# Five buffered weight pieces before each norm, the inversion's matrix in another pool, and later sums behind the mixer

## The chip, the cores and the metric

The kernel runs on one core of a Trainium2 chip. The metric is the device time of one execution in microseconds (us), taken as the median over runs; lower is better.

## What is computed

A decoder trunk of two layers works on 264 tokens: one prompt of 256 and eight samples of one token each, in float32, 1024 channels wide. Each layer is

```python
h = LN1(alpha*x + 0.5*SwiGLU_1(x))
h = LN2(alpha*h + W_out [DeltaNet(h) | Pool(h)])
x = LN3(alpha*h + 0.5*SwiGLU_2(h))
```

A SwiGLU has gate and up matrices of 1024 x 2816 and a down matrix of 2816 x 1024. The mixer projects `h` with one matrix (q, k, v, z, pooling input and two small gates), runs a gated delta rule in exact chunked form (which needs the inverse of a triangular matrix per head and chunk) beside a causal pooling, and projects both with `W_out`. States of the samples are read and written.

## The kernel before, in words

**Products.** Channels lie on the partitions and the 264 tokens along the free dimension. A float32 product is made of three matmuls per block of 128 channels (`mm3`, lines 218 to 222): each weight piece of 128 output channels is split into a rounded high part and a low remainder, each activation likewise, and high x high, high x low and low x high are summed. A piece has 8 blocks, so 24 matmuls.

**Weights.** `Weights` (line 139) holds an ordered list of units. A unit is one load of 1 MB on SP's queue into a buffer `wraw` (three of them) and holds two pieces. ScalarE writes a piece's high part (`whi`, L179) and VectorE the low part (`wlo`, L184). Three pieces have buffers in the pool `wpool` (`WB = 3`). Four more (`XB = 4`) have buffers `xhi0`, `xlo0` and so on in the pool `xp` at the right end of the memory, which is open only from the end of one stage to the start of the next. The list of units (lines 206 to 215) says which units ahead of a norm use them: the first two gate/up units (not in the very first SwiGLU) and the first two units of `w_in`. `W.ahead(n)` loads until n pieces are ready or on their way; `W.after` and `W.after_hi` name an instruction behind which the planner has to put the next low and high parts.

**Norms.** Ahead of a norm's result the next stage already works: `RH` and `RL` are high and low parts of the unnormalised rows times the gain, and `raw_products` (line 399) multiplies them with the first pieces. `Norm.stats` (line 335) sums over channels on TensorE from two accumulators `acc1`, `acc2`; `normalise` (line 355) then subtracts the mean (L360), multiplies by the reciprocal deviation (L363), scales (L365) and makes `HH` (L367) and `HL` (L375), which all later products read. `settle` (line 416) corrects the early products with mean and deviation. In the first SwiGLU of the second layer and in both SwiGLUs behind a mixer there are six early products; in these last two the order on TensorE is: three products up to block 5, the sums of `stats`, the fourth product up to block 5, then blocks 6 and 7 of all four, then the fifth and sixth products, and then a pair of products on `HH` and `HL`. In a mixer the four k pieces are early, and the pair (first q, last pooling group) with the small gates follows on `HH` and `HL`.

**Behind the mixer.** The loop at line 1244 makes the eight tiles of `W_out` and calls `norm.add`, which at high priority adds the tile to `X` (L332), makes squares (L267), `RH` (L269), `RL` (L270) and the running sums on VectorE (L277, L278, L280, L282).

**Order of the work.** TensorE runs in program order. On the other engines a planner orders the instructions by a simulation: of those that are ready, the one with the higher priority, and then the one that comes first in the program, goes first. The order is fixed when the kernel is built, and each engine then waits at its next instruction. SP's loads are one such queue.

**Pools.** `ffn` opens a pool `fp` with `gh` and `gl`, 22 rows each, whose widths and offsets come from `ROWS`. The mixer has a pool `mp`, and, once `xp` is closed, a pool `mp2` at the right end, in the place of `xp`. `MT`, the matrix to be inverted (6 KB per partition), is in `mp`; its place serves `uw` later. Buffers of one pool that reuse memory of another wait for its last user, tile by tile.

Of the kernel before, what the change touches and what calls it, by code (L numbers as in the profile page):

```python
# [9 lines left out]
F32 = mybir.dt.float32  # L10
F32R = mybir.dt.float32r
AF = mybir.ActivationFunctionType
ALU = mybir.AluOpType
# [3 lines left out]
P = 128  # L17
# [8 lines left out]
H = 4  # L26
# [6 lines left out]
WB = 3  # L33
XB = 4
SB = 3
ROWS = ((320, 0), (288, 0), (320, 16), (272, 0))
IDLE = 18
# [53 lines left out]
def trunk(ctx: ExitStack, tc: tile.TileContext, a: dict):  # L91
# [30 lines left out]
    def tables(name):  # L122
        tc.keep_in_program_order(nc.scalar.preload_act_table_set(name))
# [84 lines left out]
    for l in range(DEPTH):  # L208
        for n in ("f1", "f2"):
            for m in range(KF):  # L210
                units.append((a[n + "_gu"][l, m], 2 * m if m < 2 and (l, n) != (0, "f1") else None))
            units += [(a[n + "_d"][l, i], None) for i in range(KF // 2)]
            if n == "f1":
                units += [(a["w_in"][l, i], 2 * i if i < 2 else None) for i in range(10)]
                units += [(a["w_out"][l, i], None) for i in range(4)]
# [24 lines left out]
    class Norm:  # L240
# [4 lines left out]
        def __init__(self, l, which, eps, fold=True):  # L245
            self.l, self.eps, self.fold = l, eps, fold
            c = S_LN + 16 * which
            self.c = c
            self.g = lambda m: sm[:, l, c + m:c + m + 1]
            self.b = lambda m: sm[:, l, c + 8 + m:c + 9 + m]  # L250
            self.acc1 = lpool.tile([P, T], F32, name="acc1", tag="acc1")
            self.acc2 = lpool.tile([P, T], F32, name="acc2", tag="acc2")
            self.shift = None

        def columns(self):
# [6 lines left out]
        def shifted(self, m, eng1, eng2):  # L262
            y = X[:, m, :]
            sq = lpool.tile([P, T], F32, name="sq", tag="sq", bufs=4)
            late = self.fold and m > 5
            if not late:
                nc.scalar.activation(sq, y, AF.Square)  # L267
            if self.fold:
                self.rh_op = nc.scalar.activation(RH[:, m, 0:T], y, AF.Copy, scale=self.g(m))  # L269
                self.rl_op = nc.vector.scalar_tensor_tensor(RL[:, m, 0:T], y, self.g(m), RH[:, m, 0:T].bitcast(F32),  # L270
                                                            ALU.mult, ALU.subtract)
            if late:
                nc.scalar.activation(sq, y, AF.Square)
# [54 lines left out]
        def add(self, m, ps):  # L328
            if m == 0:
                self.columns()  # L330
            with tc.high_priority():
                nc.vector.tensor_add(X[:, m, :], ps, X[:, m, :])  # L332
                self.shifted(m, nc.vector, nc.vector)

# [20 lines left out]
        def normalise(self):  # L355
# [6 lines left out]
            for n, y in enumerate(pairs):  # L362
                nc.vector.tensor_mul(y, y, by2(self.rstd))  # L363
                for m in (2 * n, 2 * n + 1):
# [60 lines left out]

    def ffn(src, norm, xnext, rows, late=False):
        with tc.tile_pool(name="fp", bufs=1, reuse_waits="tile") as fp:
            rs, room = rows
            if room:
                fp.tile([P, room], F32, name="room")  # L430
            gh, gl = ([fp.tile([P, rs], F32R, name=f"{n}{m}")[:, 0:T] for m in range(KF)] for n in ("gh", "gl"))

# [13 lines left out]
            if src is not None:  # L446
# [3 lines left out]
                                                 [((0, 1), 0, 4), None, ((0, 1), 4, KD), ((2, 3), 0, KD), ((4, 5), 0, KD)])  # L450
                W.after, W.after_hi = src.rstd_op, src.exp_op
                src.normalise()
                tables("silu_and_others")
                W.ahead(2)
# [40 lines left out]
    def mixer(l, src, norm, xstack):  # L495
        with tc.tile_pool(name="mp", bufs=1, reuse_waits="tile") as mp:
# [51 lines left out]
            src.normalise()  # L548
            kr = [k_raw(p) for p in pk_]
            xstack.close()  # L550
            W.xp = None
# [69 lines left out]


            W.ahead(2)
            wq, wp = W.get(), W.get()
            pq, pp, pba = (psa.tile([P, T], F32, name=n, tag="ax") for n in ("pq", "pp", "pba"))
            for k in range(KD):
                nc.tensor.matmul(pba, wb[:, k, :], HH[:, k, :], start=k == 0, stop=False)
                nc.tensor.matmul(pba, wb[:, k, :], HL[:, k, :], start=False, stop=k == KD - 1)
                mm3(pq, wq, k, HH[:, k, :], HL[:, k, :], k == 0, k == KD - 1)
                mm3(pp, wp, k, HH[:, k, :], HL[:, k, :], k == 0, k == KD - 1)  # L630
            bar = mp.tile([8, 3 * P], F32, name="bar")
# [124 lines left out]

            MT = mp.tile([P, H, 3 * P], F32, name="MT")

# [443 lines left out]
            sf = mp.tile([P, NB, P], F32, name="sf", tag="S", bufs=SB)[:, 0:H]  # L1202
            uw = mp.tile([P, 2, H, P], F32, name="uw", tag="MT")
            for b in range(2):
# [84 lines left out]
    for l in range(DEPTH):  # L1289
        n1 = Norm(l, 0, 4.0 * LN_EPS)  # L1290
        ffn(src, n1, True, ROWS[2 * l])
        n2 = Norm(l, 1, LN_EPS)
        mixer(l, n1, n2, xstack)
        src = Norm(l, 2, 4.0 * LN_EPS, l < DEPTH - 1)
        ffn(n2, src, l < DEPTH - 1, ROWS[2 * l + 1], True)
    src.stats()
# [93 lines left out]
```

## Time and profile before

| | us |
|---|---|
| median of 3 runs | 1102.72 |
| lowest, highest | 1101.37, 1105.08 |
| the profiled execution, its own time | 1104.32 |
| its span, first to last instruction | 1102.2 |
| TensorE busy in it | 1049.1 |
| VectorE busy | 766.0 |
| ScalarE busy | 581.8 |

TensorE is busy for 95% of the span. It stands for some 14 us at the end, behind the last matmul, and for the rest in short gaps around the norms and within the mixers. A busy share is an average over stages: the SwiGLUs keep TensorE busy without a gap, while near the norms VectorE is full for stretches of 15 to 20 us.

### The profile page before, as it was taken

Reading aid. Unit: us, or ns where it says so; the run is one execution under the profiler, and the core shown is the slowest. Engines: PE = TensorE matmul, PEld = TensorE weight load, DVE = VectorE, ACT = ScalarE, POOL = GpSimd, SP = SyncE. Lnnn points to the kernel's source line nnn. Section 1 sums busy time; section 2 is a strip of 40 time slices with the busy share of each in tenths; the row PEclk is TensorE's granted clock in tenths of the full one; section 3 lists DMA queues with packets and bytes.
Section 4 is the critical chain, followed back from the end, with each engine's and each line's share of the span. In section 5 each row is a group of like instructions: output and inputs, shape, how many; then the busy total and the mean of one; then the engine's idle time right before and its main releaser. Section 6 shows DMA issues by size and latency. Waiting matters only on the chain.

```text
span 1102.2 us, 20763 instructions
## 1 busy us (share of the span) xinstructions
PE 1049.1 (95%) x8410; PEld 1034.9 (94%) x8410; DVE 766.0 (70%) x1226; ACT 581.8 (53%) x1017; POOL 208.0 (19%) x248
## 2 busy tenths in 40 slices
PE   8999999989898999999999999999799989999995
PEld 8999999988898999999999999998789989999994
DVE  5555567899789855557775555778997897555554
ACT  5444445657546644445564444456564466444432
POOL 0000022244940000004100000322567200000132
PEclk9999999999999999999999999999899999999998
DMA  8455445642224354554615455565331344554441
GB/s 305 181 190 188 171 178 199 228 147 98 100 115 181 117 186 179 189 190 165 257 63 205 169 178 190 191 241 170 128 118 47 146 163 158 187 192 176 169 154 40
DMA packets 35872, 183.24 MB, mean 166 GB/s; under 512 B 6848, under 2 KB 12608, under 8 KB 15552
## 3 DMA queue, kind: packets, MB, share of 16 engines
q1 hardware_dynamic: 28704, 175.19, 43.7%
q10 hardware_dynamic: 7072, 6.72, 1.8%
q8 instruction: 66, 1.08, 0.4%
q14 instruction: 30, 0.25, 0.1%
HBM read 175.18 MB, written 6.72 MB: 165 GB/s over the span
## 4 chain that ended last, share of the span: by engine, by line
PE 79%; DVE 11%; ACT 5%; POOL 3%; issue 1%; DMA 1%; ACTq 0%; DVEq 0%
PE pd L221 8%; PE pd L220 8%; PE pd L222 8%; PE pu L222 7%; PE pg L221 7%; PE pg L222 7%; PE pu L220 7%; PE pu L221 7%; PE pg L220 7%; DVE wlo L184 2%; ACT X L365 2%; POOL X L326 1%; DVE c L525 1%; ACT whi L179 1%; ACT HH L367 1%
## 5 line engine op out<-in xcount | busy, mean ns | idle before, releaser
L184 DVE TENSOR_TENSOR wlo<-wraw,whi 128x1024 fp32r<-128x1024 f32 (+1 forms) x306 | 374.1, 1226 | 214.7 <-ACT whi L179 214.0
L179 ACT ACTIVATE whi<-wraw 128x1024 fp32r<-128x1024 f32 (+1 forms) x306 | 317.6, 1041 | 337.6 <-issue 115.0
L221 PE MATMUL pd<-gl,whi 128*128 128x264 f32 x704 | 199.5, 283 | 0.0
L220 PE MATMUL pd<-gh,whi 128*128 128x264 f32 x704 | 199.2, 283 | 0.0
L222 PE MATMUL pd<-gh,wlo 128*128 128x264 f32 x704 | 199.2, 283 | 0.0
L220 PE MATMUL pu<-HH,whi 128*128 128x264 f32 x632 | 180.5, 286 | 3.1 <-ACT whi L179 3.1
L222 PE MATMUL pu<-HH,wlo 128*128 128x264 f32 x632 | 179.9, 285 | 2.2 <-DVE wlo L184 2.2
L220 PE MATMUL pg<-HH,whi 128*128 128x264 f32 x632 | 180.1, 285 | 1.4 <-ACT whi L179 1.3
L222 PE MATMUL pg<-HH,wlo 128*128 128x264 f32 x632 | 180.2, 285 | 0.4 <-DVE wlo L184 0.4
L221 PE MATMUL pg<-HL,whi 128*128 128x264 f32 x632 | 179.8, 285 | 0.0
L221 PE MATMUL pu<-HL,whi 128*128 128x264 f32 x632 | 179.8, 284 | 0.0
L222 PEld LDWEIGHTS pd<-gh,wlo 128*128 128x128 f32 x704 | 132.4, 188 | 0.0
L220 PEld LDWEIGHTS pd<-gh,whi 128*128 128x128 f32 x704 | 132.3, 188 | 0.0
L221 PEld LDWEIGHTS pd<-gl,whi 128*128 128x128 f32 x704 | 132.2, 188 | 0.0
L300 POOL TENSOR_TENSOR s<-X 128x264 fp32r<-128x264 f32 x4 | 3.0, 761 | 646.6 <-DVE X L297 646.6
L220 PEld LDWEIGHTS pu<-HH,whi 128*128 128x128 f32 x632 | 119.9, 190 | 3.7 <-ACT whi L179 3.7
L222 PEld LDWEIGHTS pu<-HH,wlo 128*128 128x128 f32 x632 | 119.2, 189 | 2.9 <-DVE wlo L184 2.9
L220 PEld LDWEIGHTS pg<-HH,whi 128*128 128x128 f32 x632 | 119.6, 189 | 1.8 <-ACT whi L179 1.8
L222 PEld LDWEIGHTS pg<-HH,wlo 128*128 128x128 f32 x632 | 119.3, 189 | 0.9 <-DVE wlo L184 0.7
L221 PEld LDWEIGHTS pu<-HL,whi 128*128 128x128 f32 x632 | 120.0, 190 | 0.0
L221 PEld LDWEIGHTS pg<-HL,whi 128*128 128x128 f32 x632 | 119.7, 189 | 0.0
L439 DVE TENSOR_TENSOR gt<-sg,pu 128x264 f32<-128x264 f32 x79 | 33.9, 429 | 50.7 <-PE pu L222 50.4
(375 smaller groups left out, 2043.8 us busy)
## 6 DMA issues: line engine op xcount, KB each, us to landing
wraw<-in_f_gu SPq DMA_DIRECT2D x86, 1024.0 KB, 4.8
wraw<-in_f_d SPq DMA_DIRECT2D x44, 1024.0 KB, 4.8
wraw<-in_w_in SPq DMA_DIRECT2D x20, 1024.0 KB, 5.0
wraw<-in_w_out SPq DMA_DIRECT2D x8, 1024.0 KB, 4.8
S<-in_sdelta SPq DMA_DIRECT2D x8, 512.0 KB, 5.2
out_o_ds<-S ACTq DMA_DIRECT2D x8, 512.0 KB, 2.6
X<-in_xT ACTq DMA_DIRECT2D x4, 264.0 KB, 5.5
wraw<-in_f_gu SPq DMA_DIRECT2D x4, 256.0 KB, 7.1
```

What stands on the lines that cost most here:

```text
L179: self.last_hi = nc.scalar.activation(h, r, AF.Copy)
L184: nc.vector.tensor_sub(l, r, h.bitcast(F32))
L220: nc.tensor.matmul(ps, hi[:, k, :], xh, start=first, stop=False)
L221: nc.tensor.matmul(ps, hi[:, k, :], xl, start=False, stop=False)
L222: nc.tensor.matmul(ps, lo[:, k, :], xh, start=False, stop=last)
L300: nc.gpsimd.tensor_add(self.s2, X[:, 0, :], X[:, 1, :])
L326: nc.gpsimd.tensor_sub(X[:, m, :], X[:, m, :], self.shift)
L365: nc.scalar.activation(X[:, m, :], X[:, m, :], AF.Identity, scale=self.g(m), bias=self.b(m))
L367: nc.scalar.activation(h, y, AF.Copy)
L439: nc.vector.tensor_mul(gt, sg, u)
L525: nc.vector.scalar_tensor_tensor(c[:, d:SEQ], y[:, 0:SEQ - d], cw(j, 3 - d), c[:, d:SEQ], ALU.mult, ALU.add)
```

## The change

- `XB` is 5: the first five pieces ahead of a norm use buffers in `xp`, so the third unit has its first piece there and its second in `wpool`.
- In the mixer the pair of products on `HH`, `HL` that uses the fifth piece comes in the program before `xp` is closed. The order on TensorE is the same.
- `MT` and `uw` move from `mp` to `mp2`.
- `gh` and `gl` have rows of 264 elements, without `ROWS`.
- In `Norm.add` only the addition to `X`, `RH` and `RL` are of high priority; squares come behind `RH`, and squares and sums have the priority of their place in the program.
- In a SwiGLU behind a norm the low parts of the next two pieces are put behind the last multiplication by the deviation (L363) instead of behind the deviation (L131).

```diff
-XB = 4
+XB = 5
-ROWS = ((320, 0), (288, 0), (320, 16), (272, 0))
...
-                units.append((a[n + "_gu"][l, m], 2 * m if m < 2 and (l, n) != (0, "f1") else None))
+                units.append((a[n + "_gu"][l, m], 2 * m if m < 3 and (l, n) != (0, "f1") else None))
...
-                units += [(a["w_in"][l, i], 2 * i if i < 2 else None) for i in range(10)]
+                units += [(a["w_in"][l, i], 2 * i if i < 3 else None) for i in range(10)]
...
             late = self.fold and m > 5
-            if not late:
+            if not late and not self.behind_weights:
                 nc.scalar.activation(sq, y, AF.Square)
             if self.fold:
-                self.rh_op = nc.scalar.activation(RH[:, m, 0:T], y, AF.Copy, scale=self.g(m))
-                self.rl_op = nc.vector.scalar_tensor_tensor(RL[:, m, 0:T], y, self.g(m), RH[:, m, 0:T].bitcast(F32),
-                                                            ALU.mult, ALU.subtract)
-            if late:
+                with tc.high_priority() if self.behind_weights else nullcontext():
+                    nc.scalar.activation(RH[:, m, 0:T], y, AF.Copy, scale=self.g(m))
+                    self.rl_op = nc.vector.scalar_tensor_tensor(RL[:, m, 0:T], y, self.g(m), RH[:, m, 0:T].bitcast(F32),
+                                                                ALU.mult, ALU.subtract)
+            if late or self.behind_weights:
                 nc.scalar.activation(sq, y, AF.Square)
...
         def add(self, m, ps):
             if m == 0:
                 self.columns()
+            self.behind_weights = True
             with tc.high_priority():
                 nc.vector.tensor_add(X[:, m, :], ps, X[:, m, :])
-                self.shifted(m, nc.vector, nc.vector)
+            self.shifted(m, nc.vector, nc.vector)
...
-                nc.vector.tensor_mul(y, y, by2(self.rstd))
+                self.y_op = nc.vector.tensor_mul(y, y, by2(self.rstd))
...
-            rs, room = rows
-            if room:
-                fp.tile([P, room], F32, name="room")
-            gh, gl = ([fp.tile([P, rs], F32R, name=f"{n}{m}")[:, 0:T] for m in range(KF)] for n in ("gh", "gl"))
+            gh = [fp.tile([P, T], F32R, name=f"gh{m}") for m in range(KF)]
+            gl = [fp.tile([P, T], F32R, name=f"gl{m}") for m in range(KF)]
...
-                W.after, W.after_hi = src.rstd_op, src.exp_op
                 src.normalise()
+                W.after, W.after_hi = src.y_op, src.exp_op
...
             kr = [k_raw(p) for p in pk_]
+
+            W.ahead(2)
+            wq, wp = W.get(), W.get()
+            pq, pp, pba = (psa.tile([P, T], F32, name=n, tag="ax") for n in ("pq", "pp", "pba"))
+            for k in range(KD):
+                nc.tensor.matmul(pba, wb[:, k, :], HH[:, k, :], start=k == 0, stop=False)
...
             xstack.close()
             W.xp = None
...
-            W.ahead(2)
-            wq, wp = W.get(), W.get()
...
-            MT = mp.tile([P, H, 3 * P], F32, name="MT")
+            MT = mp2.tile([P, H, 3 * P], F32, name="MT")
...
-            uw = mp.tile([P, 2, H, P], F32, name="uw", tag="MT")
+            uw = mp2.tile([P, 2, H, P], F32, name="uw", tag="MT")
```

## Rows read from the trace of the kernel before

**Rows 1.** The page, busy time, share of the span and instructions of each engine

```profile
PE 1049.1 (95%) x8410; PEld 1034.9 (94%) x8410; DVE 766.0 (70%) x1226; ACT 581.8 (53%) x1017; POOL 208.0 (19%) x248
```

**Rows 2.** Waits of PE: total us, times, longest us

```profile
PE pq L222 <- DVE wlo L184: 8.3, 2, 4.1
...
PE pu L222 <- DVE xlo L184: 5.5, 2, 2.8
...
PE pu L220 <- ACT whi L179: 3.1, 3, 1.1
PE pu L222 <- DVE wlo L184: 2.2, 3, 0.8
```

**Rows 3.** Busy time by stretch: PE, PEld, DVE, ACT, POOL, clock, DMA, GB/s

```profile
400.00:410.00 10.00, 10.00 (x86) 10.00 (x85) 5.56 (x8) 5.03 (x8) 0.00 (x0) 1.00 0.58 210
219.00:233.50 14.50, 9.93 (x81) 9.48 (x79) 14.45 (x40) 9.64 (x27) 5.28 (x5) 0.99 0.37 120
233.50:238.00 4.50, 4.48 (x25) 4.48 (x26) 4.50 (x13) 0.24 (x1) 2.45 (x2) 0.65 0.48 169
...
333.00:352.74 19.74, 16.54 (x131) 15.91 (x130) 19.49 (x41) 14.79 (x27) 0.00 (x0) 1.00 0.36 136
...
369.40:373.40 4.00, 3.98 (x20) 3.98 (x21) 2.94 (x6) 2.75 (x8) 0.00 (x0) 0.57 0.69 246
...
566.80:571.30 4.50, 4.50 (x25) 4.50 (x26) 4.37 (x12) 1.17 (x5) 0.00 (x0) 0.62 0.69 233
...
203.50:206.20 2.70, 2.70 (x21) 2.57 (x20) 0.24 (x2) 0.54 (x3) 1.31 (x4) 1.00 0.98 399
```

**Rows 4.** Timeline of DVE before the norm's sums, first layer: start, us

```profile
346.93 0.43 DVE L280 TENSOR_TENSOR acc<-acc,X 128x264 f32<-128x264 f32 x1
...
348.99 1.22 DVE L184 TENSOR_TENSOR xlo<-wraw,xhi 128x1024 fp32r<-128x1024 f32 x1
...
352.74 2.35 DVE L184 TENSOR_TENSOR wlo<-wraw,whi 128x1024 fp32r<-128x1024 f32 x2
```

**Rows 5.** Timeline of PE there: the stand, and the norm's sums

```profile
350.26 0.39 PE L222 MATMUL pu<-RH,xlo 128*128 128x266 f32 x1 [2.75 <-DVE xlo L184]
...
354.58 0.61 PE L339 MATMUL ps<-acc,cst 128*128 128x264 f32 x2
```

**Rows 6.** Timeline of DVE within that norm

```profile
359.58 1.22 DVE L184 TENSOR_TENSOR wlo<-wraw,whi 128x1024 fp32r<-128x1024 f32 x1
360.72 2.56 DVE L363 TENSOR_TENSOR X<-X,rstd 128x528 f32<-128x528 f32 x4
```

**Rows 7.** Timelines of ACT and PE at the end of the early products

```profile
367.07 1.04 ACT L179 ACTIVATE whi<-wraw 128x1024 fp32r<-128x1024 f32 x1
...
368.16 0.39 PE L220 MATMUL pu<-HH,whi 128*128 128x264 f32 x1 [1.03 <-ACT whi L179]
...
369.42 0.39 PE L222 MATMUL pu<-HH,wlo 128*128 128x264 f32 x1 [0.75 <-DVE wlo L184]
```

**Rows 8.** Timelines of DVE and PE at the mixer's start, first layer

```profile
200.99 1.44 DVE L184 TENSOR_TENSOR wlo<-wraw,whi 128x1024 fp32r<-128x1024 f32 x1 [0.54 <-ACT whi L179]
...
223.26 1.22 DVE L184 TENSOR_TENSOR wlo<-wraw,whi 128x1024 fp32r<-128x1024 f32 x1
...
205.02 0.61 PE L339 MATMUL ps<-acc,cst 128*128 128x264 f32 x2
...
233.52 0.59 PE L222 MATMUL pq<-HH,wlo 128*128 128x264 f32 x1 [4.15 <-DVE wlo L184]
```

**Rows 9.** Loads of the samples' states: SP's timeline and waits, landing, first reader

```profile
202.10 19.87 SPq L832 DMA_DIRECT2D S<-in_sdelta  x4
...
SPq L832 <- PE pk L222: 13.5, 2, 6.8
...
S<-in_sdelta SPq DMA_DIRECT2D x8, 512.0 KB, 5.2
...
220.54 0.62 ACT L850 ACTIVATE RH<-S 128x512 fp32r<-128x512 f32 x1
```

More of the change, by code (lines that the diff above doesn't have):

```diff
@@ L253, in __init__ @@
             self.shift = None
+            self.behind_weights = False
         def columns(self):
@@ L423, in settle, with ffn @@
             return y, c[:, 1:2]
-    def ffn(src, norm, xnext, rows, late=False):
+    def ffn(src, norm, xnext, late=False):
         with tc.tile_pool(name="fp", bufs=1, reuse_waits="tile") as fp:
-            rs, room = rows
-            if room:
-                fp.tile([P, room], F32, name="room")
-            gh, gl = ([fp.tile([P, rs], F32R, name=f"{n}{m}")[:, 0:T] for m in range(KF)] for n in ("gh", "gl"))
+            gh = [fp.tile([P, T], F32R, name=f"gh{m}") for m in range(KF)]
+            gl = [fp.tile([P, T], F32R, name=f"gl{m}") for m in range(KF)]
             def gate(m, y, bias, u, ubias):
@@ L549, in mixer @@
             kr = [k_raw(p) for p in pk_]
+            W.ahead(2)
[3 more added lines that the diff above has]
+                nc.tensor.matmul(pba, wb[:, k, :], HH[:, k, :], start=k == 0, stop=False)
+                nc.tensor.matmul(pba, wb[:, k, :], HL[:, k, :], start=False, stop=k == KD - 1)
+                mm3(pq, wq, k, HH[:, k, :], HL[:, k, :], k == 0, k == KD - 1)
+                mm3(pp, wp, k, HH[:, k, :], HL[:, k, :], k == 0, k == KD - 1)
             xstack.close()
@@ L620, in p_map @@
                 return finish
-            W.ahead(2)
-            wq, wp = W.get(), W.get()
[L625 to L630, printed above, removed]
             bar = mp.tile([8, 3 * P], F32, name="bar")
@@ L1290, in trunk @@
         n1 = Norm(l, 0, 4.0 * LN_EPS)
-        ffn(src, n1, True, ROWS[2 * l])
+        ffn(src, n1, True)
         n2 = Norm(l, 1, LN_EPS)
@@ L1294, in trunk @@
         src = Norm(l, 2, 4.0 * LN_EPS, l < DEPTH - 1)
-        ffn(n2, src, l < DEPTH - 1, ROWS[2 * l + 1], True)
+        ffn(n2, src, l < DEPTH - 1, True)
     src.stats()
```

## The prediction
> **What bounds the kernel now.** I read the busy shares first: TensorE works for 95% of the span [rows 1], so time can only come from its stands, its clock and its end. The list of its waits comes next [rows 2]. Four entries belong to places that the change touches: a q product of the mixer waits for the low part of its piece (8.3 us in two waits, one per layer); the second early up-product behind each mixer waits for its low part (5.5 us, two waits); and the first products on normalised rows wait for the high part (3.1 us, three waits) and then the low part (2.2 us, three waits) of their second piece. The three places are the SwiGLUs behind the two mixers and the first one of layer two. Third, the table by stretches [rows 3] says what stands behind each wait, by whether VectorE is full, and what the clock does after it.
>
> **Mixer's start.** VectorE works 14.45 of 14.50 us before the wait of 4.15 us ends [rows 3, 8]; it is the bound there. Among its work is the split at 223.26, 1.22 us long. It is the eighth piece's: with pieces five to seven in the three ordinary buffers, the eighth must wait until the pair of products has freed one. With a fifth extra buffer, pieces six to eight take the ordinary ones, and the eighth can be split beside the early k products. Between 203.50 and 206.20 VectorE works 0.24 of 2.70 us, so there is room. Everything behind 223.26 then moves forward by 1.22 us, and as VectorE stays full up to the wait, so does TensorE. Gain: 2 x 1.22 = 2.4 us. Bounds: nothing, if the planner leaves the split where it is; 2 x 4.15 = 8.3 us, if the low part that ends the wait overtakes the convolutions too. I take the first-named sum, as the change does not alter that part's priority. The moved split may cost more: the one at 200.99 took 1.44 us while GpSimd was at work, against 1.22 us [rows 8]. Even so it fits into the idle 2.46 us.
>
> The Trainium skill, SBUF — State Buffer, section "SBUF: two separate sides", has a harsher rule: a VectorE instruction with two SBUF inputs and a GpSimd instruction that reads SBUF lock each other out for a whole instruction. A split is such an instruction, and the moved one would then stand behind one of the small GpSimd products of that stretch; at worst, by my estimate from that page, it is half a microsecond longer than in the quiet stretch, reaches into the norm's sums at 205.02, and the total gain is about 0.4 us less. The row agrees in direction, and shows 0.22 us.
>
> **Behind the mixer, the sums.** From 333.00 to 352.74 VectorE works 19.49 of 19.74 us [rows 3]. The running sums, like the one at 346.93, go first, and the low part at 348.99 comes behind them; TensorE stands 2.75 us for it [rows 4, 5]. In the changed kernel that piece comes earlier in the program than all but the first of the sums and no longer has a lower priority, so it goes first. VectorE has the same work, so the stand is not removed but moved: TensorE reaches the norm's sums early, and they need the last accumulator. What VectorE does up to 352.74 contains all sums and all four extra low parts; the two splits at 352.74 (2.35 us) come later in the program than the sums and can stay behind them. So the sums can start at 352.74 instead of 354.58 [rows 4, 5]: 1.84 us per layer, 3.7 us in all. A stand of about 0.9 us is left in front of them: without the 2.75 us TensorE would be there at 351.83. Bounds per layer: 2.75 us gained, if VectorE finds a gap I don't see; 0.5 lost, if the two splits go before the sums (352.74 + 2.35 = 355.1 against 354.58).
>
> **The pair on normalised rows.** Its second piece gets its high part at 367.07, when the early products have freed a buffer; TensorE waits 1.03 us for it and 0.75 us for the low part [rows 7]. With the extra buffer both pieces of the pair find ordinary buffers free from the start, so the high parts come right behind the deviation. The added order (low parts behind the last multiplication by the deviation) makes no engine wait for another, as both are on VectorE; behind the low parts stand the low halves `HL` and the corrections of the early products. Is it in time? At 352.74 VectorE still has the two splits and the work of the norm. The norm's last multiplication now ends at 360.72 + 2.56 = 363.28, with one split (359.58, 1.22 us) before it [rows 6]. That split now goes behind, and the sums come 1.84 us sooner, so with no stand it could end at 360.2; as VectorE must also do the two splits from 352.74, I take 361.5. Two low parts (2.4 us) end at 363.9, and with one low half between at 364.6. TensorE comes to the pair 1.84 us before 367.13, that is at 365.3. The wait goes at all three places: 3.1 + 2.2 = 5.3 us [rows 2]. Next late is `HL` of the last rows, which the pair needs only in its last quarter.
>
> **The clock.** After two of these stands rows show the clock at the lower of its levels (1.2 and 2.4 GHz) for part of a stretch: 20 matmuls in 3.98 us at a mean of 0.57, and 25 in 4.50 us at 0.62 [rows 3]. At the steady pace, 86 in 10 us [rows 3], they take 2.33 and 2.91 us. What came before was in both cases a stand of 1.8 us, broken by two matmuls. If the stand goes, I count these 1.65 + 1.59 = 3.2 us as given back. After the wait in the mixer the clock is low too (25 matmuls in 4.48 us, 0.65) [rows 3]; as 2.9 us of that wait are left, I count nothing.
>
> **At no cost:** the move of `MT` and of the pair in the program (TensorE's order is unchanged, and five buffers of 8 KB and the mixer's later pool with `MT` fill the same 40 KB); the narrower rows of `gh` and `gl`, since these are written long after the mixer's buffers in their place are done with.
>
> **Sum.** 2.4 + 3.7 + 5.3 + 3.2 = 14.6 us. The profiled execution took 1104.32 us, 2.1 more than its span and 1.6 more than the median; it would take 1089.7, and the median of 1102.72 becomes **1088.1 us**. About 0.3% (3.3 us) is what a measurement of this kernel can tell from no change.
>
> **Rivals.**
> 1. *The stand moves to the sums in full.* The planner, whose loads may land earlier than the chip's, puts the two splits before the sums: 0.5 us lost instead of 1.84 gained, in both layers, 4.7 us less: 1092.8. For it: VectorE is full there, and any split that goes first delays the sums. Against it: the sums come first in the program.
> 2. *The pair still waits.* The low parts now stand behind the last multiplication and compete with `HL` and the corrections; if these go first, the low parts come no sooner than now, and stand and clock (5.3 + 3.2) remain: 14.6 - 8.5 = 6.1 us gained, 1096.6. For it: `HL` comes earlier in the program. Against it: `HL` waits for ScalarE between its parts, which leaves VectorE time for a split.
> 3. *Slower: a state load that stands too long.* `MT` shifts the later buffers of the right pool by 6 KB, among them the one for the first head's states. Of the four loads, issued from 202.10 to 221.97, one waits 6.8 us for a k product; if its new place lay on the fifth piece, it would be issued at 221.97 and land 5.2 us later, at 227.2, while ScalarE reads the states from 220.54 [rows 9]. ScalarE would stand for 6.6 us, with convolutions, pooling inputs and the next high parts queued behind it, VectorE and then TensorE after it. The 2.4 us of the mixer are lost, 13.2 us are added, and two more stretches at the low clock cost 3.2: 14.6 - 2.4 - 13.2 - 3.2 = -4.2, so 1106.9. It decides if ScalarE stands over 4.5 us per layer. Against it: the load waits for a k piece now, and 6 KB is less than a piece of 8 KB, so I expect the next k piece, whose product ends before the pair begins.
>
> **Chances.** Forecast 0.56; rival 1 0.17; rival 2 0.13; rivals 1 and 2 together (about 1.4 us gained) or a change without effect 0.07; rival 3 0.06; the mixer's whole wait gone as well 0.01. So faster 0.87, within 0.3% 0.07, slower 0.06. The range reaches from 1082 (the mixer's wait gone: 5.9 us more) to 1098 (rival 2, with 1.2 us of the mixer's gain missing).
>
> **What would show it.** Right: no wait of `pu` for `xlo` or for the pair's second piece; the list of waits has a new entry of about 0.9 us per layer, of the sums on `acc`; granted clock 1.00 behind the pair; the q wait near 2.9 us with a split fewer behind 222. Rival 1: the sums wait over 3 us, the `wlo` splits in front of them. Rival 2: splits behind `HL`. Rival 3: ScalarE idle before L850 on a load. The prediction is wrong if the down products, 86 matmuls in 10 us now, run at another pace.

## The result, and the profile after

| | before | changed |
|---|---|---|
| median on the same chip, us | 1103.90 (4 runs) | 1089.33 (4 runs) |
| lowest, highest | 1101.37, 1107.47 | 1087.61, 1091.58 |
| the profiled execution, its own time | 1104.32 | 1089.43 |
| its span | 1102.2 | 1087.6 |

The ratio is 0.9861, with an interval of 0.9826 to 0.9895: 14.6 us faster. The forecast was 1088.1 us, by a gain of 14.6 us. The total agrees; its terms agree less well, and that is what the rest is about.

The page of the changed kernel has the busy line that answers to [rows 1]. The work is the same, and the span is shorter around it:

```profile
PE 1046.0 (96%) x8410; PEld 1030.9 (95%) x8410; DVE 765.6 (70%) x1226; ACT 581.8 (53%) x1016; POOL 205.9 (19%) x248
```

The list of TensorE's waits in the changed kernel (total us, times, longest us) answers to [rows 2]. None of the four entries shown there is left:

```profile
PE py L624 <- DVE dm L620: 6.2, 2, 3.2
PE pst L908 <- POOL parts L906: 5.6, 2, 2.8
PE ps L341 <- DVE acc L281: 2.8, 2, 1.4
PE pdiff L706 <- DVE gm L702: 2.1, 2, 1.2
...
PE pp L221 <- DVE wlo L183: 1.2, 2, 0.6
...
PE py L624 <- PE pp L221: 0.5, 2, 0.3
```

Four of these are new: the norm's sums wait for the accumulator, `pdiff` for `gm`, `pp` for a low part, and `py` a little for `pp`. The wait of `py` for `dm` was there before, shorter:

```profile
PE py L615 <- DVE dm L611: 4.5, 2, 2.3
```

So the mixer's q wait of 8.3 us did not shrink to 5.9 as forecast; it went, and 1.7 + 2.1 + 1.2 + 0.5 = 5.5 us came back under other names.

The timeline of VectorE in the changed kernel, at the mixer's start (first two lines, against [rows 8]), behind the mixer (next five, against [rows 4]) and at the pair on normalised rows (last four, against [rows 6, 7]); the columns are start, duration, engine and line:

```profile
200.73 1.80 DVE L183 TENSOR_TENSOR wlo<-wraw,whi 128x1024 fp32r<-128x1024 f32 x1
202.45 1.21 DVE L183 TENSOR_TENSOR wlo<-wraw,whi 128x1024 fp32r<-128x1024 f32 x1
...
347.76 1.22 DVE L183 TENSOR_TENSOR xlo<-wraw,xhi 128x1024 fp32r<-128x1024 f32 x1
348.89 0.42 DVE L278 TENSOR_TENSOR acc<-X 128x264 f32<-128x264 f32 x1
...
353.36 0.43 DVE L283 TENSOR_TENSOR acc<-acc,sq 128x264 f32<-128x264 f32 x1
353.70 1.23 DVE L183 TENSOR_TENSOR xlo<-wraw,xhi 128x1024 fp32r<-128x1024 f32 x1
354.84 1.23 DVE L183 TENSOR_TENSOR wlo<-wraw,whi 128x1024 fp32r<-128x1024 f32 x1
...
361.44 1.33 DVE L365 TENSOR_TENSOR X<-X,rstd 128x528 f32<-128x528 f32 x2
362.67 1.23 DVE L183 TENSOR_TENSOR wlo<-wraw,whi 128x1024 fp32r<-128x1024 f32 x1
363.81 0.71 DVE L377 TENSOR_TENSOR HL<-X,HH 128x528 fp32r<-128x528 f32 x1
364.43 1.23 DVE L183 TENSOR_TENSOR wlo<-wraw,whi 128x1024 fp32r<-128x1024 f32 x1
```

The reader is to see three things. Ahead of the norm's sums VectorE now has two splits, at 200.73 and 202.45, where the kernel before has one there (at 200.99). Behind the mixer the split at 347.76 precedes all sums, the sums stand without a gap, and the two last splits follow them. At the pair both low parts come right behind the last multiplication, with one low half of the rows between.

The timeline of TensorE in the changed kernel shows where it now stands (the time in brackets is the idle time before, with its releaser):

```profile
205.10 0.61 PE L341 MATMUL ps<-acc,cst 128*128 128x264 f32 x2
...
252.75 0.69 PE L624 MATMUL py<-dm,pw 128*128 128x264 f32 x2 [3.25 <-DVE dm L620]
...
284.79 0.47 PE L908 MATMUL pst<-cst,parts 128*128 128x128 f32 x1 [2.81 <-POOL parts L906]
...
353.50 0.71 PE L341 MATMUL ps<-acc,cst 128*128 128x264 f32 x2 [1.40 <-DVE acc L281]
```

And the table by stretches of the changed kernel, in the columns of [rows 3]:

```profile
220.00:234.50 14.50, 13.46 (x107) 12.86 (x107) 14.46 (x45) 9.38 (x26) 4.72 (x6) 1.00 0.29 86
280.00:290.00 10.00, 7.19 (x45) 6.82 (x44) 5.77 (x11) 3.81 (x9) 10.00 (x14) 0.83 0.06 25
348.89:353.50 4.61, 3.21 (x26) 2.99 (x25) 4.61 (x15) 1.54 (x4) 0.00 (x0) 1.00 0.62 242
362.00:368.00 6.00, 6.00 (x51) 6.00 (x50) 6.00 (x10) 6.00 (x12) 0.00 (x0) 1.00 0.14 52
```

VectorE is still full from 220 on. TensorE is busy without a gap at the pair, at full clock. New is the clock of 0.83 behind `pst`: the stand there is as long as before, but after it the clock fell.

**The stretches.** A stretch here runs from the first start of one TensorE output to the first start of another, by the timeline, so a shift handed on from earlier cancels. The columns give both layers where there are two numbers: the mixer's start (`pba` to the first `psq`), `pst` to `pskt`, behind the mixer (`pout` to `ps`), the SwiGLU behind it (`ps` to its first down product `pd`), and `ps` to `pd` of the first SwiGLU of layer two. Each row is one profiled execution, in us, under the name that its experiment has below:

| kernel | start | pst to pskt | pout to ps | ps to pd | layer two's first SwiGLU |
|---|---|---|---|---|---|
| before | 45.56, 45.73 | 9.10, 10.91 | 23.29, 23.30 | 126.10, 124.61 | 129.88 |
| rows_264 | 45.76, 44.88 | 10.91, 9.10 | 23.31, 25.98 | 124.61, 126.12 | 128.39 |
| changed | 44.30, 43.70 | 11.32, 10.92 | 21.23, 21.23 | 122.37, 122.36 | 126.02 |
| same_again | 43.73, 44.31 | 9.10, 11.32 | 21.25, 21.25 | 122.35, 122.36 | 126.02 |
| sums_as_before | 42.74, 43.71 | 9.10, 10.91 | 25.97, 23.30 | 122.25, 122.25 | 126.02 |
| four_pieces | 45.82, 44.90 | 9.10, 9.09 | 21.25, 21.25 | 125.19, 125.19 | 127.66 |
| w_in_four | 45.76, 45.75 | 9.10, 9.10 | 21.22, 21.24 | 122.37, 122.36 | 126.02 |
| low_parts_before_rstd | 45.45, 44.30 | 11.33, 9.10 | 21.23, 21.23 | 122.65, 122.62 | 126.02 |

From before to changed: 1.26 + 2.03 = 3.3 us at the mixers' starts, 2.06 + 2.07 = 4.1 behind them, 3.73 + 2.25 + 3.86 = 9.8 in the SwiGLUs; against that 2.2 lost behind `pst`. That makes 15.0 us; the spans differ by 14.6, so 0.4 us more was lost elsewhere (from `pd` to the next `ps` the first SwiGLU of layer two took 68.67 us in the profiled execution of the kernel before, 69.34 in that of the changed one and in rows_264).

### The profile page after: what moved, and what is told of

It reads as the page before. It is cut to its first block, busy times and chain, and to the rows that moved or that the text cites. A ratio compares the mean times of both kernels' runs of the same rounds, so it can differ in the third digit from the quotient of the medians.

```text
span 1087.6 us, 20766 instructions
## 1 busy us (share of the span) xinstructions
PE 1046.0 (96%) x8410; PEld 1030.9 (95%) x8410; DVE 765.6 (70%) x1226; ACT 581.8 (53%) x1016; POOL 205.9 (19%) x248
## 4 chain that ended last, share of the span: by engine, by line
PE 82%; DVE 10%; ACT 3%; POOL 2%; issue 1%; DMA 1%; ACTq 0%; DVEq 0%
PE pd L219 8%; PE pd L221 8%; PE pd L220 8%; PE pu L220 8%; PE pu L219 8%; PE pu L221 8%; PE pg L220 7%; PE pg L219 7%; PE pg L221 7%; DVE wlo L183 2%; POOL X L327 1%; DVE c L525 1%; ACT X L367 1%; DMA wraw<-in_f_gu 1%; PE pout L220 1%
## 5 line engine op out<-in xcount | busy, mean ns | idle before, releaser
L183 DVE TENSOR_TENSOR wlo<-wraw,whi 128x1024 fp32r<-128x1024 f32 (+1 forms) x301 | 369.9, 1231 | 203.8 <-ACT whi L178 203.0
L178 ACT ACTIVATE whi<-wraw 128x1024 fp32r<-128x1024 f32 (+1 forms) x301 | 312.5, 1041 | 318.7 <-issue 116.9
```

Of the source, the lines that this page charges most:

```text
L178: self.last_hi = nc.scalar.activation(h, r, AF.Copy)
L183: nc.vector.tensor_sub(l, r, h.bitcast(F32))
```

## The experiments

Times are medians. Kernels are compared by their ratios to the kernel before, which ran beside them on the same chip; the names are those of the table above.

**The changed kernel once more** (same_again, no edit).

> The changed kernel again, unaltered, to see what moves between two executions of one program. Theory: in the first layer's mixer the changed kernel lost about 2.2 us between 285 and 296 us because the stand of 2.8 us there (a transpose of stacked keys waiting for GpSimd) was followed by a stretch at the lower clock, and that this is a matter of when the execution falls, not of the change; so the loss may be there or not in this execution, and the median stays at 1089 (ratio 0.986). Rival: the change itself lengthens that stretch; then the first layer's distance from that transpose to the next one of the sums is again 11.3 us, and 9.1 us in the kernel before.

Measured: 1088.20 us (5 runs) beside 1105.56 (14 runs), ratio 0.9845 [0.9825, 0.9866]. The low clock behind `pst` was absent in layer one and present in layer two. The table by stretches of this execution, layer one and then layer two:

```profile
284.00:293.00 9.00, 8.66 (x66) 8.31 (x67) 5.56 (x13) 4.04 (x9) 9.00 (x13) 1.00 0.00 0
815.00:824.00 9.00, 8.32 (x47) 7.34 (x47) 4.56 (x8) 2.12 (x5) 9.00 (x13) 0.81 0.00 0
```

66 matmuls against 47 in 9 us, by one program, after the same stand of 2.81 us. So the loss behind `pst` is not a cost that the change always brings: a stand is a chance of low clock, and the table of stretches shows it in kernels of either kind.

**The sums as before** (sums_as_before).

```diff
         def add(self, m, ps):
...
-            self.behind_weights = True
             with tc.high_priority():
                 nc.vector.tensor_add(X[:, m, :], ps, X[:, m, :])
-            self.shifted(m, nc.vector, nc.vector)
+                self.shifted(m, nc.vector, nc.vector)
```

> The changed kernel with the squares and sums behind the mixer at high priority again, and squares ahead of RH. Theory (the stand only moves from the second up-product to the norm's sums, and what is won is the two splits that VectorE no longer does ahead of the sums, 1.5 to 2 us per layer): the wait of 2.75 us for xlo is back in both layers, the wait of the sums for acc is gone, and the time is 3 to 4.5 us above the changed kernel, 1092 to 1094. Rival (a moved stand is worth nothing): within 1 us of the changed kernel, 1089.

Measured: 1092.32 us (5 runs), 0.9881 [0.9862, 0.9900]; some 4 us above the changed kernel on the same chip. Its list of waits has the early up-product again and no wait of the sums:

```profile
PE pu L221 <- DVE xlo L183: 5.5, 2, 2.8
```

The stretch behind the mixer took 23.30 us in layer two, 2.07 more than in the changed kernel, and 25.97 in layer one, where the clock fell around the stand, as the table by stretches shows:

```profile
345.00:352.00 7.00, 4.38 (x20) 4.38 (x21) 7.00 (x11) 1.38 (x2) 0.00 (x0) 0.63 0.47 165
```

The edit of the sums is worth 2.07 us per layer, and more whenever the longer stand costs the clock.

**Four pieces again** (four_pieces), the rest of the change kept.

```diff
-XB = 5
+XB = 4
```

> The changed kernel with XB = 4, so that the fifth piece uses an ordinary buffer again; all else (pools, rows, sums, low parts behind the last multiplication) as changed. Theory (the fifth buffer is what takes away the stand before the pair of products on normalised rows, at three places, and gives the mixer's start 1.2 us per layer): waits of the pair's second piece for high and low parts of 1.8 us at three places, the q wait of about 4 us in both layers, the lower clock behind one or two of the pairs; 8 to 11 us above the changed kernel, 1097 to 1100. Rival (the order behind the last multiplication and the sums do the work): 1090 to 1093, without these waits.

Measured: 1100.08 us (9 runs, 1095.51 to 1104.34), 0.9947 [0.9924, 0.9971]; 11.9 above the changed kernel on that chip. The list of waits:

```profile
PE pq L221 <- DVE wlo L183: 8.3, 2, 4.1
...
PE pu L219 <- ACT whi L178: 3.3, 3, 1.5
...
PE pu L221 <- DVE wlo L183: 2.3, 3, 0.8
```

The three waits of [rows 2] that the fifth buffer was to remove are back to within 0.2 us, while the stretch behind the mixer stays at 21.25. So the two parts of the change act apart, and the buffer is the larger. The mixers' starts (45.82, 44.90) are those of the kernel before with narrow rows (45.76, 44.88), so the moves of `MT` and of the pair, which this kernel keeps, give or cost nothing there by themselves. The profiled execution was the fastest of the nine, with full clock behind the pairs. The 9 us between the nine go with the mean granted clock of each run: 0.989 in the two fastest (1095.51 and 1095.72 us), 0.981 and 0.980 in the two slowest (1104.34 and 1104.03).

**Four pieces for the mixer alone** (w_in_four): the mixer's input weights get no fifth buffer, the gate and up pieces keep it.

```diff
-                units += [(a["w_in"][l, i], 2 * i if i < 3 else None) for i in range(10)]
+                units += [(a["w_in"][l, i], 2 * i if i < 2 else None) for i in range(10)]
```

> The changed kernel with the fifth piece in an extra buffer for gate and up only; w_in has four as before. Theory (VectorE is full at the mixer's start, so that one split moved ahead of it is worth its 1.2 us, and what the q wait lost beyond that came back as waits for dm and gm): the q wait of about 4 us is back and the waits for dm shorter; from the pair's first product to the first transpose of squared keys 1.2 us more per layer, 2.4 us in all, 1091.7. Rival 1 (the whole q wait is a gain): 8 us more, 1097. Rival 2 (the stretch is full whatever comes first): no difference, 1089.3.

Measured: 1088.74 us (4 runs), 0.9853 [0.9834, 0.9872]. The q wait is back in full; its line in the list of waits is that of four_pieces, 8.3 us in two.

The mixers' starts took 45.76 and 45.75 us, 1.5 and 2.0 more than in the changed kernel, yet the median is only 0.5 us higher, and the intervals overlap. In its profiled execution the clock did not fall behind `pst` in either layer (9.10 twice), which gives 4.0 us back against the profiled execution of the changed kernel. Whether an earlier start of the mixer makes that fall likelier stays open: the four kernels of the table whose starts all took over 44.8 us show it in 2 of 8 stretches, the other four in 5 of 8. So the mixer's part of the fifth buffer is real in its stretch and not to be seen in the medians.

**The width of the rows alone** (rows_264), in the kernel before.

```diff
-ROWS = ((320, 0), (288, 0), (320, 16), (272, 0))
+ROWS = ((264, 0), (264, 0), (264, 0), (264, 0))
```

> The kernel before with one part of the change alone: the rows of the SwiGLU's two halves are 264 elements wide in all four SwiGLUs, as in the changed kernel, and nothing else is altered. Theory: the width changes no instruction and no buffer that is waited for, so the time is that of the kernel before (within 3 us) and its waits for the pieces (pq 8.3, pu 5.5, 3.1 and 2.2 us) are all there. Rival: the old widths were there to keep buffers of neighbouring pools from waiting for each other; then a new wait shows and the time rises by more than 3 us.

Measured: 1105.14 us (10 runs) beside 1103.58 (19 runs), 1.0014 [0.9994, 1.0034], and the waits are those of before. The width does nothing. The execution is useful otherwise: with the one of before it gives each SwiGLU with the clock full and with it low (124.61 and 126.10; 128.39 and 129.88), so 1.5 us is the price of one low clock there.

**The order at the pair undone** (low_parts_before_rstd).

```diff
                 src.normalise()
-                W.after, W.after_hi = src.y_op, src.exp_op
+                W.after, W.after_hi = src.rstd_op, src.exp_op
```

> The changed kernel with one part undone: the low parts of the pair's pieces wait for the deviation alone, as in the kernel before, and no longer for the last multiplication by it. Theory (the added order is not what the gain comes from; the fifth buffer is, and the pair has about 2 us to spare): VectorE does the two low parts (2.4 us) ahead of some multiplications or among them, TensorE's waits at the pair stay away or are under 0.5 us, and the time is that of the changed kernel within 2 us. Rival: the low parts hold up the normalised rows, TensorE waits for HH or HL at the pair at three places, and 2 to 7 us are lost.

Measured: 1087.94 us (4 runs) beside 1104.74 (9 runs), 0.9849 [0.9824, 0.9874], the changed kernel's ratio. One low part now runs ahead of the multiplications behind the mixers, which end 0.7 us later counted from the sums, and the SwiGLUs behind the mixers take 0.3 us longer. So the buffer does the work at the pair; the added order is worth 0.3 us in two places.

**The running sums of X on GpSimd** (sums_on_gpsimd).

```diff
-            self.shifted(m, nc.vector, nc.vector)
+            self.shifted(m, nc.gpsimd, nc.vector)
```

> The changed kernel with the running sums of X behind the mixer on GpSimd (the sums of the squares stay on VectorE). Theory (behind the mixer VectorE's work in full sets when the norm's sums start, and the new stand of 1.4 us per layer is what is left of it): seven additions leave VectorE per layer, the stand of the sums on the accumulator goes, and the kernel gains 2 to 3 us against the changed one. Rival (a VectorE instruction and a GpSimd one with two operands in SBUF slow each other down): the splits and additions of VectorE beside GpSimd's sums become longer, GpSimd's own sums end last, and nothing is gained, or up to 4 us are lost.

Measured: 1097.45 us (8 runs) beside 1103.58, 0.9944 [0.9923, 0.9965]; some 11 us slower than the changed kernel by the ratios. First the list of waits, then the timelines of GpSimd (first line) and VectorE behind the mixer:

```profile
PE ps L342 <- DVE acc L283: 8.3, 2, 4.1
```

```profile
346.91 0.87 POOL L281 TENSOR_TENSOR acc<-acc,X 128x264 f32<-128x264 f32 x1 [0.78 <-DVE X L334]
...
347.09 1.77 DVE L183 TENSOR_TENSOR xlo<-wraw,xhi 128x1024 fp32r<-128x1024 f32 x1
...
350.67 1.21 DVE L183 TENSOR_TENSOR xlo<-wraw,xhi 128x1024 fp32r<-128x1024 f32 x1
...
352.15 1.21 DVE L183 TENSOR_TENSOR wlo<-wraw,whi 128x1024 fp32r<-128x1024 f32 x1
353.29 2.04 DVE L283 TENSOR_TENSOR acc<-acc,sq 128x264 f32<-128x264 f32 x4
```

Two things show. A split that starts while a GpSimd addition runs takes up to 1.77 us instead of 1.21, as the rival has it. And the planner now puts the splits at 350.67 and 352.15 ahead of the last sums of squares, so the stand grows to 4.1 us: the prediction's first rival, brought about by another edit. The granted clock then reads 0.66 from 355 to 360:

```profile
355.00:360.00 5.00, 3.57 (x16) 3.39 (x17) 4.18 (x9) 1.76 (x4) 0.00 (x0) 0.66 0.47 193
```

From `pout` to `pd` a layer takes 147.9 and 148.0 us, 143.6 in the changed kernel. Of these 4.3 us the longer stand is 2.7 (4.1 less 1.4), and the low clock behind it is about what is left. How much of the stand is owed to the slower splits and how much to their order, the run does not tell.

**Two state splits later** (state_low_part_late): in the mixer's start, the low parts of the first two states go behind the pooling's last difference.

```diff
+            marks = {}
...
-                    nc.vector.tensor_sub(dm[:, 0:16], dm[:, 0:16], ext[:, 15:31])
+                    marks["dm"] = nc.vector.tensor_sub(dm[:, 0:16], dm[:, 0:16], ext[:, 15:31])
...
-                nc.vector.tensor_sub(lo, s, hi.bitcast(F32))
+                with behind(marks["dm"] if h < 2 and x == 0 else None):
+                    nc.vector.tensor_sub(lo, s, hi.bitcast(F32))
```

> The changed kernel with the low parts of the first two states (first half of each, 2.75 us of VectorE in the full stretch ahead of the scores) put behind the last difference that the pooling's products wait for. Theory (VectorE, full from the start of the mixer on, is the bound there, and the q wait that went came back as the longer wait of the pooling's first product, 6.2 us in two waits): that wait becomes 1 to 2.7 us shorter per layer, and 2 to 5 us are gained in all. Rival 1: the work comes back before the scores or in the first level of the inversion, and the time stays within 2 us of the changed kernel. Rival 2: the wait is not set by VectorE's work but by its order, and nothing changes at the pooling's first product.

Measured: 1086.94 us (5 runs), 0.9843 [0.9812, 0.9874], no different from the changed kernel. The list of waits says why:

```profile
PE pst L910 <- POOL parts L908: 7.0, 2, 3.5
PE py L625 <- DVE dm L621: 4.0, 2, 2.0
```

The pooling's first product waits 1.1 us less per layer, as the theory has it, and `pst` 0.7 us more: counted from `psq`, the subtraction on GpSimd that it waits for starts 1.1 us later (27.9 and 27.8 us, 26.8 in the changed kernel). The mixers' starts fell to 41.07 and 42.62 us, the first of them in part because no low clock followed the pooling's wait in that layer; rival 1 holds for the time.

**The parts early** (parts_early): the subtraction of GpSimd that `pst` waits for gets a higher priority.

```diff
-                nc.gpsimd.tensor_sub(pt[:, :, 2 - i, :], hb(src_), pt[:, :, 0, :])
+                with tc.high_priority(): nc.gpsimd.tensor_sub(pt[:, :, 2 - i, :], hb(src_), pt[:, :, 0, :])
```

> The changed kernel with higher priority for one subtraction of GpSimd (0.25 us), which the transposition pst waits for: it now stands before six of the eight shifts of X, where it stood behind all of them and behind four products of N. Theory: the stand of 2.8 us per layer at pst goes, and with it the low clock that follows it in some executions (about 2 us where it comes): 5 to 9 us gained; the planner also puts two splits ahead of the sums behind the mixer, which may give back up to 2 us per layer. Rival 1: the four products of N, now 0.25 us later, or the states behind them, are the next thing that TensorE waits for, and the stand only moves: under 2 us. Rival 2: the order behind the mixer outweighs it, and the time does not fall.

Measured: 1082.64 us (4 runs) beside 1103.58, 0.9808 [0.9777, 0.9838]. The list of waits no longer has `pst`; the states' products `psk` wait a little more (1.9 us, 1.0 in the changed kernel):

```profile
PE psk L861 <- DVE RL L851: 1.9, 4, 0.7
```

GpSimd's timeline shows the subtraction, which started at 284.49 in the changed kernel:

```profile
275.19 0.74 POOL L327 TENSOR_TENSOR X<-X,shift 128x264 f32<-128x264 f32 x1
275.89 0.25 POOL L906 TENSOR_TENSOR parts<-dec,parts 128x32 f32<-128x32 f32 x1
276.11 6.02 POOL L327 TENSOR_TENSOR X<-X,shift 128x264 f32<-128x264 f32 x5
```

From `psq` to `pskt` a layer takes 34.1 us; the changed kernel took 36.2 without the low clock and 38.0 to 38.4 with it. So 2.1 us per layer are gained, or about 4 where the clock would have fallen. By the ratios it is some 4 us against same_again, under the 5 expected: of the 5.6 us of the two stands 0.9 come back at `psk`. The two splits that I expected ahead of the sums did not come: VectorE's order behind the mixer is that of the changed kernel, and `pout` to `ps` is 21.23 as there.

**Both edits together** (parts_and_state).

> The changed kernel with both edits that the runs so far favour: the subtraction for pst ahead of six shifts of X, and the low parts of the first two states behind the pooling's differences. Theory: with the late low parts alone, what was won at the pooling's first product (1.3 to 2.7 us per layer) was lost again at pst, where GpSimd's work ends at its own time; with pst's wait gone both gains stand, 2 to 4 us less than with the subtraction alone, so 1078 to 1081 us. Rival: VectorE's late low parts come back in front of the inversion (the waits on the states grow), and the time is that of the subtraction alone (1081 to 1084 us).

Measured: 1082.83 us (5 runs) beside 1104.74, 0.9788 [0.9763, 0.9814]. The rival's time, and its wait: `psk` on the states has grown.

```profile
PE psk L863 <- DVE RL L853: 3.4, 6, 0.7
```

In the traces nothing is left of the late low parts. From `pba` to `pskt` both layers take 78.3 us; with the subtraction alone they take 79.2 and 78.0, and the 79.2 is the layer in which the clock was low for longer (a mean of 0.51 from 252 to 259). The intervals of this kernel and of the parts early alone overlap.

**The sums one product later** (sums_one_product_later), on top of both edits.

```diff
-                raw = src.raw_products("gugugu", [((0,), 0, 6), ((1,), 0, 6), ((2,), 0, 6), None, ((3,), 0, 6),
+                raw = src.raw_products("gugugu", [((0,), 0, 6), ((1,), 0, 6), ((2,), 0, 6), ((3,), 0, 6), None,
```

> The kernel with both edits, and behind the mixer TensorE's norm sums placed behind the fourth early product instead of ahead of it (18 matmuls, 2.4 us). Theory (the stand of 1.4 us per layer at the sums is TensorE arriving too early, with other work at hand; the pair has about 2 us to spare): the stand goes, the sums come 1.0 us later than before at most, the pair does not wait, and 2.8 us are gained, so 1075 to 1078.5 us. Rival: the norm, 1 us later, is late for the pair, and the stand appears there (HH, HL or the low parts): under 1 us gained.

Measured: 1080.91 us (4 runs) beside 1104.74, 0.9781 [0.9757, 0.9804]. The stand at the sums is gone, but the pair has small ones in its place:

```profile
360.28 0.39 PE L220 MATMUL pg<-HL,whi 128*128 128x264 f32 x1 [0.37 <-DVE HL L377]
361.41 0.39 PE L221 MATMUL pu<-HH,wlo 128*128 128x264 f32 x1 [0.37 <-DVE wlo L183]
```

From `pout` to `pd` a layer takes 143.2 us, 143.6 without this edit: 0.4 us gained instead of 1.4. The pair had less to spare than I took it to have (0.56 us in the changed kernel, as shown further on), and the rival is right. This kernel has the lowest median of all; the last two kernels lie below the changed one beyond their intervals, and cannot be told from each other.

## Why the prediction was right, and where it was not

**Mixer's start**: forecast 2.4 us, by one split of 1.22 us per layer taken out of VectorE's full stretch. Measured 1.26 and 2.03, 3.3 us. The mechanism held: one split more runs ahead of the sums, and four_pieces and w_in_four bring the wait back. VectorE is the bound up to the last wait of the stretch, that of `py` for `dm`: in the changed kernel it works 29.73 of the 29.80 us from 222.80 to 252.60, with one instruction fewer than before. Counted from `pba`, TensorE goes on there after 40.70 and 40.77 us in the kernel before, after 39.32 and 38.72 in the changed one (38.92 and 39.34 in same_again): 1.38 and 2.05 us sooner. Why this is more than the 1.22 us of the split, the runs do not settle.

What failed is the picture of the wait: "as 2.9 us of that wait are left". None was left at q. These lines show the low part that q waits for, before and changed, and the last wait before (the changed one is at 252.75 above):

```profile
232.26 1.21 DVE L184 TENSOR_TENSOR wlo<-wraw,whi 128x1024 fp32r<-128x1024 f32 x1
...
228.15 1.21 DVE L183 TENSOR_TENSOR wlo<-wraw,whi 128x1024 fp32r<-128x1024 f32 x1
...
254.05 0.78 PE L615 MATMUL py<-dm,pw 128*128 128x264 f32 x1 [2.27 <-DVE dm L611]
```

At 228.15 the low part runs ahead of five convolutions that stood before it at 232.26, although the change leaves its priority alone. It did overtake other VectorE work, and that work was then late for `dm`, `gm` and `pp`: of the 8.3 us 5.5 came back. The low clock behind the q wait went with it, but TensorE still waited 2.27 us for `dm` behind that low clock, so it was not the bound there. The upper bound of 8.3 looked at one wait only, where VectorE is full for the whole stretch and what is owed is paid later.

The moved split met GpSimd, as the prediction had weighed. GpSimd's lines in the changed kernel:

```profile
200.68 0.76 POOL L281 TENSOR_TENSOR acc<-acc,X 128x264 f32<-128x264 f32 x1 [4.33 <-DVE X L295]
...
202.72 1.17 POOL L511 TENSOR_TENSOR pre<-scT,sm 128x96 f32<-128x96 f32 x1 [1.05 <-DMA scT<-in_sconv]
```

The split at 200.73 started 0.05 us behind GpSimd's addition and took 1.80 us, 0.58 longer than the quiet 1.22. The split at 202.45 started first and took 1.21; GpSimd's product at 202.72 then took 1.17, and 0.57 in the kernel before. In sums_on_gpsimd a split that started 0.18 us behind an addition of 0.87 us took 0.56 longer. In these lines the one of the two that starts second takes longer, by some 0.6 us. It cost the sums nothing, as the splits ran ahead of them: they started at 205.10 against 205.02 [rows 8]. These lines agree with the lock for a whole instruction that the Trainium skill, SBUF — State Buffer, section "SBUF: two separate sides", has between the two engines, and the half microsecond that I worked out from it was right in size.

**Behind the mixer**: forecast 1.84 us per layer with a stand of 0.9 us left. Measured 2.06 and 2.07 with a stand of 1.40. The order of sums and splits was as forecast, and sums_as_before confirms it. Counted from `pout`, the sums came 0.22 us earlier than forecast (353.50 less the 0.98 us by which `pout` was late there, against 352.74), and TensorE 0.71 earlier (352.10 less 0.98, against 351.83), which makes the longer stand. Of the 0.71, 0.36 is the small wait of the output product for its low part, which went too. The rest is what a stand costs beyond the idle time in its bracket (0.27 us, worked out at the pair below): 0.27 for each of the two stands that went, less 0.16, because the bracket of the new one begins only when the last matmul has ended (0.28 long, at a step of 0.12). That gives 0.36 + 0.54 - 0.16 = 0.74.

**The pair**: forecast 5.3 us of waits and 3.2 of clock. Measured 9.8. By the executions with full clock (124.61 and 128.39) the waits were worth 2.25 + 2.25 + 2.37 = 6.9, the clock 1.49 + 1.49 = 3.0. The term mis-sized is the stand: 1.78 us by its rows, 2.3 in the stretch. These lines of the kernel before, on either side of the matmul at 368.16 [rows 7], show why:

```profile
366.85 0.28 PE L222 MATMUL pg<-HH,wlo 128*128 128x264 f32 x1
...
368.39 0.28 PE L221 MATMUL pu<-HL,whi 128*128 128x264 f32 x1
```

From 366.85 to 368.39 are two steps, 1.54 us; at the steady pace (86 in 10 us) a step is 0.12. So 1.30 us were lost where the bracket has 1.03: a stand costs about 0.27 us more than its idle time. For the two stands at the pair that is 1.78 + 0.54 = 2.3 us.

**The clock**: the step "if the stand goes, I count these as given back" held for the two stands that went. What was left out is that stands which stay can lose the clock too: 2.2 us behind `pst` in layer one, where the execution of before had none. The gains over forecast (0.9 + 0.4 + 1.3) and this loss cancel nearly, so the agreement of the total to 0.1 us is in part luck. As the clock term came from one execution and was taken off a median, it had an uncertainty of its own that the sum did not show; rows_264, the same instructions, had its low clocks in other places. The 14 runs of the kernel before beside same_again show the same by their mean granted clocks: the fastest took 1101.73 us at 0.988, the slowest 1110.45 at 0.978, so their spread goes with the clock.

**The rivals**: the stand moved to the sums by half, not in full. The pair did not wait, but it had little to spare. Its second low part ended at 364.43 + 1.23 = 365.66, and the first product that reads it started 0.56 us later (first line below). For rival 3 the prediction expected the state load to wait for the next k piece. It did not: in the changed kernel SP's loads of the states wait for the pair (second line, 16.8 us per layer), and the last two were issued at 221.72 and 222.10, in the kernel before at 209.81 and 221.64. Yet ScalarE has no wait for them, since its second read of the states now stands at 227.60 (third line), where it stood at 224.84. That this part of the forecast held is luck: the reason given for it was wrong.

```profile
366.22 0.28 PE L221 MATMUL pu<-HH,wlo 128*128 128x264 f32 x1
...
SPq L832 <- PE pba L556: 33.4, 2, 16.8
...
227.60 0.63 ACT L850 ACTIVATE RH<-S 128x512 fp32r<-128x512 f32 x1
```

## What to carry to other kernels

When an engine is full over a stretch, taking one instruction out is worth about its duration, however long the wait that names it; look up who waits next on that engine, and expect the named wait to move there. Price a stretch between two fixed points in several executions, since here stands of 1.8 to 2.8 us brought the low clock in some and not in others. And follow a wait on an engine that is mostly idle to its queue: here a subtraction of 0.25 us stood behind 10 us of work that nothing waited for yet, and moving it gained more than the mixer's buffer.

## What was not expected of the hardware

The same stand of 2.81 us at `pst`, in one program, was followed by full clock in one layer and by 0.81 over 9 us in the other; the price was 1.8 to 2.2 us (9.10 against 10.91 to 11.33). What decides it, the runs do not show. The stand of 2.75 us behind the mixer did the same: 23.3 us without, 26.0 with the low clock.
